# A two-part product at full TensorE load: the second weight part made by ScalarE and an accumulating transfer instead of VectorE

## The chip, the cores and the metric

One Trainium2 chip, one core of it. The metric is the device time of one execution in microseconds. The core has TensorE (matrix products, PE in the profile, PEld its weight loads), VectorE (DVE), ScalarE (ACT), GpSimd (POOL) and SyncE (SP), each with its own instruction stream, and 16 DMA engines that they share. Traces come from the hardware profiler.

## What is computed

Two layers of a generator block with four parallel branches (neighbourhood attention, pooling, grouped attention, convolution), over 256 latent tokens and, in layer 0, 256 context tokens as well; D is 2048. The weights make the bulk of the work: a combined input projection, four branch products with merge gates, and an output product.

```python
for l in range(DEPTH):
    shift, scale, gate = jnp.split(jax.nn.silu(c) @ w_ada[l] + b_ada[l], 3, axis=-1)
    h = modulate(x, g_pre[l], shift[:, None], scale[:, None])
    p = split_proj(h @ w_in[l])
    ...                                            # branches o_a, o_b, o_c, o_d
    y = branch_merge(p, o_a, o_b, o_c, o_d, w_branch[l], w_out[l])
    x = x + gate[:, None] * rms_norm(y, g_post[l])
```

## The kernel before

All products are of 32-bit numbers, and each operand is split in two parts, hi and lo, whose sum is the number. One product becomes three passes of TensorE: hi weights by hi activations, hi weights by lo activations, lo weights by hi activations (`mm3`, lines 164 to 167). The weights therefore arrive as a raw tile and are split on the chip.

The main stream is a list of *units*, each one raw weight tile of up to 1 MB (128 x 2048), and *steps*, each one half of a unit (128 x 1024): 24 passes of TensorE. In layer 0 the steps 96 to 165 are the input projection, 166 to 335 the four merges (pairs of a 1 MB unit of two steps for the gate, a 512 KB unit of one step for the branch product of two columns, and another 1 MB unit). In the steps of layer 0 a product mostly covers 512 columns, in layer 1 256.

`run` writes the order of every engine out by hand. Ahead of the products of step j it issues:

- `hi_op` for up to step j+3: ScalarE copies the raw half into a `wh` tile (line 279), a pool of four (`NHI`);
- `lo_op` for up to step j+2: VectorE subtracts, `wl = raw - wh` (line 286), a pool of three (`NLO`);
- behind the `lo_op` of a unit's last half, `dmas`: the raw tile of a unit that comes later, on SP's queue (line 237). There are three raw tiles (`NRAW`), and the load waits until the tile's earlier contents have been read;
- then the evacuation of the previous step (`post`), and ahead of each half of the step's products one or two *pulls*: pieces of side tasks (attention, convolution, pooling) and of a back task, the adaLN columns on VectorE (`ada_task`, from line 1051), which load 256 KB tiles `aw` on SP's queue (line 1061) one pull before VectorE multiplies them (lines 1098 and 1100).

Every engine takes its instructions in that order and waits where a tile is not ready or a buffer not free. GpSimd has next to nothing to do. PSUM has eight banks, from one pool.

Of the kernel before, what the change touches and what calls it, by code (L numbers as in the profile page):

```python
# [10 lines left out]
F32 = mybir.dt.float32  # L11
F32R = mybir.dt.float32r
AF = mybir.ActivationFunctionType
# [17 lines left out]
# column tiles of w_in, in the order in which the kernel consumes them  # L31
# [21 lines left out]
# columns of the table of per-feature parameters of a layer  # L53
# [9 lines left out]
class Step:  # L63
    __slots__ = ("unit", "half", "mm", "post", "pre", "pulls", "again", "cap")

    def __init__(self, unit, half, mm, post=None, pre=None, pulls=("", ""), again=False, cap=1.9):
        # again: the weights of this step are those that an earlier step of the unit has left
        # cap: the work that VectorE can take on in a pull, in us
        self.unit, self.half, self.mm, self.post, self.pre = unit, half, mm, post, pre
        self.pulls, self.again, self.cap = pulls, again, cap  # L70


class Unit:
    def __init__(self, src, widths, raw="raw", split="w", keep=False):
        # raw, split: where the loaded tile and its parts live; "u" is the common pool of 2 KB tiles
        # keep: a later step uses the parts again
        self.src, self.widths, self.keep = src, widths, keep
        self.rpool, self.spool = raw, split
        self.raw = None
        self.hi = {}  # L80
        self.lo = {}


class Kernel:
# [5 lines left out]
    EARLY = (6, 14)  # L90

# [20 lines left out]
    # ---- allocation  # L112
# [25 lines left out]
    # ---- small helpers  # L138
    def defer(self, fn):
        # emitted at the next quarter of a unit, so that an engine need not wait for what precedes it  # L140
        self.dq.append(fn)
# [6 lines left out]
    def spend(self, w):  # L148
        # one more operation of VectorE on w columns: is that enough for this pull?
        c = w * 0.00105 + 0.2  # L150
        self.spent += c
        if self.spent + c > self.cap:
            self.spent = 0
            return True
        return False

    def split(self, hi, lo, src, lag=False):
        # src = hi + lo exactly; both parts pass TensorE in one go each
        self.S.copy(hi, src)  # L159
        sub = lambda: self.V.tensor_tensor(lo, src, hi.bitcast(F32), ALU.subtract)  # L160
        self.defer(sub) if lag else sub()
# [23 lines left out]
    def tok_sums(self, acc, T, out):  # L185
        # out[:, 2j:2j+2] = the sum over partitions of token tile j, tokens on partitions
        accs = acc if isinstance(acc, list) else [acc]
        for j in range(T // 128):
            for i, a in enumerate(accs):
                self.T.matmul(out[:, 2 * j:2 * j + 2], a[:, j * 128:(j + 1) * 128], self.ones[:, 0:2],  # L190
                              start=i == 0, stop=i == len(accs) - 1)

    def tok_bcast(self, r, T, out, step=2):
        # out[p, t] = r[t] for every partition p
        for j in range(T // 128):
            self.T.matmul(out[:, j * 128:(j + 1) * 128], r[:, step * j:step * j + 1].to_broadcast([128, 128]),
                          self.ident, is_transpose=True)

    # ---- main program
# [8 lines left out]
    def pull(self, q):  # L208
        # the next piece of the first task; where that was a light one, one of the task behind it too
        i = 0  # L210
        while i < len(q):
            try:
                light = next(q[i])
            except StopIteration:
                del q[i]
                continue
            i += 1
            if not light:
                break
        return i > 0  # L220
# [18 lines left out]
    def run(self):  # L239
# [13 lines left out]
        def ahead(i, n):  # L253
            # may the split of step i be issued now? n: buffers of the pool of the weight parts
            # at the start, where the loads hold the time, what is split early would keep other work waiting
            if i >= len(prog) or i > self.j + (self.LOOK if self.j > self.SLOW else 1) or prog[i].unit.raw is None:
                return False
            if prog[i].again or prog[i].unit.spool == "u":
                return True
            # a kept tile is in use up to its last step  # L260
            return len({(id(p.unit), p.half) for p in prog[self.j:i + 1] if p.unit.spool == "w"}) <= n
# [19 lines left out]
        def lo_op(i):  # L281
            nonlocal busy
            x, h = prog[i].unit, prog[i].half
            if prog[i].again:
                return
            x.lo[h] = piece(i, self.lp, "wl", lambda d, r, k: self.V.tensor_tensor(  # L286
                d, r, x.hi[h][k].bitcast(F32), ALU.subtract))
            left[id(x)] -= 1
            if not left[id(x)]:
                busy -= x.rpool != "u"  # L290
                dmas()
# [39 lines left out]
    # ---- set-up  # L331
# [75 lines left out]
    # ---- the modulated, normalised input  # L407
# [10 lines left out]
    def startup(self):  # L418
        # scale and shift of layer 0 on TensorE, the first columns of its projection beside them
# [23 lines left out]
        def ada_post(g):  # L443
            def post():
# [3 lines left out]
                def cols():  # L448
# [7 lines left out]
                    def mods():  # L456
                        # stream 0: columns 0 and 1 of each tile, stream 1: columns 2 and 3
                        t = self.sm(16)
                        V.tensor_copy(t, pc[:, 0:16])
                        t4 = t.rearrange("p (j s h) -> p j s h", s=2, h=2)  # L460
                        V.tensor_tensor(t4[:, :, :, 0], t4[:, :, :, 0], t4[:, :, :, 1], ALU.add)
                        for i in range(2):
                            self.mod_cols(0, 2 * g + i, t4[:, 2 * i, :, 0], t4[:, 2 * i + 1, :, 0])
# [36 lines left out]
        for g in range(8):  # L500
            # between the last of a group and the first of the next, the bank of the sums serves for their columns
# [7 lines left out]
    # ---- projections  # L509
    def store(self, l, n, i, p):  # L510
        # p: PSUM tile of projection column tile i of part n
# [49 lines left out]
    def proj_mm(self, box, xh, xl, T, half, nk=8):  # L561
        # box: list to hold the PSUM tile; contraction tiles half*nk .. of the moving operand's pieces
# [18 lines left out]
    # ---- pooling branch  # L581
# [65 lines left out]
    # ---- convolution branch  # L647
# [84 lines left out]
    def conv_pw(self, l):  # L732
        # the pointwise product of the convolution branch, as a unit of the main stream
# [29 lines left out]
    # ---- attention  # L763
    def attn(self, units):
        # one pull per stage; what a stage reads was made at least one pull earlier
# [35 lines left out]
    def att_s(self, x):  # L801
        # q: the two parts of a head one above the other, kd, kl: the first and the second part of its keys, each twice
# [13 lines left out]
    def stack(self, src, w):  # L816
        # for each head of a pair, both parts of its 64 rows in one tile; the first part lies where the head lay
# [7 lines left out]
    def double(self, src):  # L825
        # for each head of a pair, the first part of its 64 rows twice, and the second part twice
# [12 lines left out]
    def vstack(self, p3, h):  # L839
        # values of a head, tokens on partitions: for each token tile the two parts side by side  # L840
# [25 lines left out]
    def att_tr(self, x, c):  # L866
        # key tiles 2c and 2c+1, both query tiles; ctx queries have only the keys of c = 1
# [81 lines left out]
    def attn_c(self, l):  # L949
# [7 lines left out]
        # tile 0: the keys of both groups, tiles 1 to 4: the queries; rows of ss: 8 query heads, then 2 groups  # L957
# [92 lines left out]
    # ---- adaLN columns on VectorE  # L1050
    def ada_task(self, kind):
# [11 lines left out]
        # sums over partitions as rows of one bank, a row for each group and stream  # L1063
# [71 lines left out]
    # ---- layers  # L1135
# [32 lines left out]
    def values(self, l, g):  # L1168
        # four contraction tiles of the values of branch a, tokens on the partitions of the result
# [16 lines left out]
        def post():  # L1186
            # for each head the two parts of its values side by side
# [83 lines left out]
    def layer_out(self, l):  # L1271
# [17 lines left out]
        def evac(f, box, streams):  # L1289
            # streams: those in the PSUM tile, one after the other  # L1290
# [48 lines left out]
        for f in range(NK):  # L1339
            # the last tiles of layer 0: first the latents, whose sums the next layer waits for, then the context  # L1340
# [9 lines left out]
    def load_x(self, g, s):  # L1350
        # feature tiles 2g and 2g+1 of stream s
# [4 lines left out]
    def sum_up(self, key, o, t):  # L1356
        # running sums over the feature tiles
# [7 lines left out]
    def tail0(self):  # L1365
        # the residual of layer 0, then the modulated input of layer 1; feature tiles in pairs
# [31 lines left out]
        def lat_task():  # L1398
            # the sum of the squares of x + r z from the sums over x x, x z and z z
# [169 lines left out]
# ---- host side: layout only  # L1569
def _tiles(w, cols):  # L1570
    # w: (rows, n) -> for each column tile in cols: (128 partitions, rows/128 * 128)
# [4 lines left out]
def _cols(v):  # L1576
    # feature vector -> (128, n/128), feature f at partition f % 128
    return v.reshape(-1, 128).T


def layout(inp):
    f32 = np.float32
    w_in, w_ada, w_out, w_br = inp["w_in"], inp["w_ada"], inp["w_out"], inp["w_branch"]
    a = {}
# [13 lines left out]
    def ada_cols(l, cols):  # L1598
        # columns in pieces of 128 -> (16 row blocks, 128, 512)
# [31 lines left out]
    # relative position bias: gathered by indices that depend on shapes alone, padded outside the window  # L1631
# [9 lines left out]
    # constants of the shapes  # L1641
# [48 lines left out]
```

## Time and profile before

| what | before |
|---|---|
| median of two runs | 2715.28 us (2715.2 to 2715.37) |
| span of the profiled execution, first to last instruction | 2712.6 us |
| TensorE busy | 2668.9 us, 98% |
| VectorE busy | 1880.6 us, 69% |
| ScalarE busy | 1187.7 us, 44% |
| all subtractions of line 286 | 720, 779.5 us |

The profile is one execution. Its own time is known as its span alone; the runs' median stands 2.7 us above that. "Busy" counts instructions that compute; products are pipelined and their ends modelled, so two neighbours overlap in the trace. A wait is written as the instruction that stood, an arrow, and what released it. DMA share is the mean busy share of the 16 DMA engines.

### The profile page before, as it was taken

What the parts mean: (1) busy time and instruction counts of PE and PEld (TensorE: products, weight loads), DVE (VectorE), ACT (ScalarE), POOL (GpSimd) and SP (SyncE); (2) the same over time, 40 slices, a digit from 0 to 9 for tenths busy, and PEclk for the clock granted to TensorE, in tenths of its full rate; (3) what the DMA queues carried; (4) which work ended last, traced back from release to release, by engine and by line L of the source; (5) the groups of instructions that cost most, each with busy time, mean ns of one, the idle gap of its engine ahead of it and who ended that gap; (6) DMA issues with size and microseconds to landing.
All of it is one profiled execution on the core that took longest, in us unless ns stands there. A gap on an engine that the chain in (4) does not pass through costs nothing.

```text
span 2712.6 us, 38481 instructions
## 1 busy us (share of the span) xinstructions
PE 2668.9 (98%) x15468; PEld 2320.9 (86%) x15468; DVE 1880.6 (69%) x2908; ACT 1187.7 (44%) x1866; POOL 0.2 (0%) x4
## 2 busy tenths in 40 slices
PE   6999999999999999999999999999999999999997
PEld 3678888788888888888888888899999999999997
DVE  8873667886487654677787565686787876875554
ACT  7852664345422223222222233466235764664443
POOL 0000000000000000000000000000000000000000
PEclk9999999999999999999999999999999999999999
DMA  8842224442232223445455355565335545445553
GB/s 333 294 165 101 88 101 152 148 145 81 83 119 94 100 94 109 148 171 198 168 171 184 118 197 200 186 222 187 109 115 175 179 150 175 148 149 183 185 186 119
DMA packets 106307, 422.42 MB, mean 156 GB/s; under 512 B 11624, under 2 KB 22288, under 8 KB 70416
## 3 DMA queue, kind: packets, MB, share of 16 engines
q1 hardware_dynamic: 106128, 419.96, 44.5%
q8 instruction: 121, 1.98, 0.3%
q14 instruction: 58, 0.48, 0.0%
HBM read 417.82 MB, written 2.10 MB: 155 GB/s over the span
## 4 chain that ended last, share of the span: by engine, by line
PE 94%; DVE 3%; ACT 2%; DMA 1%; issue 1%; SPq 0%; DVEq 0%; ACTq 0%
PE pm L165 23%; PE pm L166 23%; PE pm L167 23%; PE pb L165 3%; PE pb L167 3%; PE pb L166 3%; PE pk L165 1%; PE pk L166 1%; PE pk L167 1%; PE pt L872 1%; PE pv L166 1%; PE pv L167 1%; PE pv L165 1%; PE pa L440 1%; PE pa L439 1%; PE o L890 1%
## 5 line engine op out<-in xcount | busy, mean ns | idle before, releaser
L286 DVE TENSOR_TENSOR wl<-raw,wh 128x1024 fp32r<-128x1024 f32 (+1 forms) x720 | 779.5, 1098 | 668.6 <-PE pm L167 456.8
L279 ACT CAST wh<-raw 128x1024 fp32r<-128x1024 f32 (+1 forms) x720 | 671.1, 951 | 1282.0 <-PE pm L166 812.8
L165 PE MATMUL pm<-hh,wh 128*128 128x512 f32 (+1 forms) x3248 | 1097.4, 338 | 0.5 <-DVE tl L160 0.4
L167 PE MATMUL pm<-hh,wl 128*128 128x512 f32 (+1 forms) x3248 | 1088.1, 335 | 0.0
L166 PE MATMUL pm<-hl,wh 128*128 128x512 f32 (+1 forms) x3248 | 1087.8, 335 | 0.0
L165 PEld LDWEIGHTS pm<-hh,wh 128*128 128x128 f32 x3248 | 616.6, 190 | 65.3 <-issue 2.2
L167 PEld LDWEIGHTS pm<-hh,wl 128*128 128x128 f32 x3248 | 616.4, 190 | 62.7
L166 PEld LDWEIGHTS pm<-hl,wh 128*128 128x128 f32 x3248 | 616.9, 190 | 60.8
L1100 DVE SCALAR_TENSOR_TENSOR aacc<-aw,sc,aacc 128x512 f32<-128x512 f32 x420 | 291.1, 744 | 1.9 <-DMA aw<-in_adaD_dram 0.8
L165 PE MATMUL pm<-yh,wh 128*128 128x256 f32 (+1 forms) x544 | 177.9, 327 | 0.0
L167 PE MATMUL pm<-yh,wl 128*128 128x256 f32 (+1 forms) x544 | 177.7, 327 | 0.0
L166 PE MATMUL pm<-yl,wh 128*128 128x256 f32 (+1 forms) x544 | 177.7, 327 | 0.0
L672 DVE SCALAR_TENSOR_TENSOR cacc<-du,hlf,cacc 128x482 f32<-128x482 f32 (+29 forms) x240 | 145.1, 605 | 5.9
L165 PEld LDWEIGHTS pm<-yh,wh 128*128 128x128 f32 x544 | 103.5, 190 | 9.1
L166 PEld LDWEIGHTS pm<-yl,wh 128*128 128x128 f32 x544 | 103.5, 190 | 8.8
L167 PEld LDWEIGHTS pm<-yh,wl 128*128 128x128 f32 x544 | 103.5, 190 | 8.7
L858 ACT ACTIVATE P<-s,sm 128x512 f32<-128x512 f32 (+1 forms) x96 | 59.2, 617 | 92.8 <-DVE sm L857 87.3
L165 PE MATMUL pk<-hh,wh 128*128 128x256 f32 (+1 forms) x240 | 81.5, 339 | 0.1
L167 PE MATMUL pk<-hh,wl 128*128 128x256 f32 (+1 forms) x240 | 80.4, 335 | 1.1 <-DVE wl L286 1.1
L166 PE MATMUL pk<-hl,wh 128*128 128x256 f32 (+1 forms) x240 | 80.6, 336 | 0.5 <-DVE hl L160 0.5
L1239 DVE SCALAR_TENSOR_TENSOR mt<-mt,pb 128x512 f32<-128x512 f32 (+1 forms) x128 | 70.5, 551 | 11.8 <-ACT mt L1236 8.8
L160 DVE TENSOR_TENSOR tl<-pt,th 128x512 fp32r<-128x512 f32 x80 | 54.8, 686 | 18.8 <-ACT th L159 18.5
(277 smaller groups left out, 2912.5 us busy)
## 6 DMA issues: line engine op xcount, KB each, us to landing
raw<-in_wm_dram SPq DMA_DIRECT2D x229, 1024.0 KB, 4.9
aw<-in_adaD_dram SPq DMA_DIRECT2D x256, 256.0 KB, 5.4
raw<-in_ada_dram SPq DMA_DIRECT2D x32, 1024.0 KB, 5.0
raw<-in_wb_dram SPq DMA_DIRECT2D x64, 512.0 KB, 3.6
raw<-in_wv_dram SPq DMA_DIRECT2D x8, 1024.0 KB, 4.9
raw<-in_wk_dram SPq DMA_DIRECT2D x8, 1024.0 KB, 5.1
xr<-in_xT_dram SPq DMA_DIRECT2D x24, 256.0 KB, 5.4
x<-in_xT_dram SPq DMA_DIRECT2D x16, 256.0 KB, 5.0
```

The costliest lines, as they stand in the source:

```text
L160: sub = lambda: self.V.tensor_tensor(lo, src, hi.bitcast(F32), ALU.subtract)
L165: mm(out, wh, xh, start=first, stop=False)
L166: mm(out, wh, xl, start=False, stop=False)
L167: mm(out, wl, xh, start=False, stop=last)
L279: x.hi[h] = piece(i, self.hp, "wh", lambda d, r, k: self.S.copy(d, r))
L286: x.lo[h] = piece(i, self.lp, "wl", lambda d, r, k: self.V.tensor_tensor(d, r, x.hi[h][k].bitcast(F32), ALU.subtract))
L439: T.matmul(pa[g][0:4, :], w, hi[i], start=rb == 0, stop=False)
L440: T.matmul(pa[g][0:4, :], w, lo[i], start=False, stop=rb == 15)
L672: V.scalar_tensor_tensor(a3[:, :, lo:hi], u3[:, :, lo + d:hi + d], hlf[:, c:c + 1], a3[:, :, lo:hi], ALU.mult, ALU.add)
L858: S.activation(P[t], ss[t], AF.Exp, scale=0.125, bias=st[:, 2 + t:3 + t], accum_out=st[:, 4 + t:5 + t])
L1100: V.scalar_tensor_tensor(accs[s], w, c, accs[s], ALU.mult, ALU.add)
L1239: V.scalar_tensor_tensor(t, t, 1.0, q, ALU.add, ALU.mult)
```

## The change

For the steps 110 to 299, where the weight parts live in the pools `wh` and `wl`, `lo_op` no longer subtracts on VectorE. ScalarE writes the negated first part into the `wl` tile, and GpSimd issues a transfer within SBUF that adds the raw half (512 KB) to it. All else, the pools, the order and the conditions, stays as it was. (Comments were taken out as well; they are left out here.)

```diff
@@ class Kernel
     EARLY = (6, 14)
+    DLO = (110, 300)
@@ lo_op
-            x.lo[h] = piece(i, self.lp, "wl", lambda d, r, k: self.V.tensor_tensor(
-                d, r, x.hi[h][k].bitcast(F32), ALU.subtract))
+            if self.DLO[0] <= i < self.DLO[1] and x.spool == "w":
+                def low(d, r, k):
+
+                    self.S.activation(d, x.hi[h][k].bitcast(F32), AF.Copy, scale=-1.0)
+                    self.G.dma_start(d, r, accum_op=ALU.add)
+                x.lo[h] = piece(i, self.lp, "wl", low)
+            else:
+                x.lo[h] = piece(i, self.lp, "wl", lambda d, r, k: self.V.tensor_tensor(
+                    d, r, x.hi[h][k].bitcast(F32), ALU.subtract))
```

## Rows read from the trace of the kernel before

**Rows 1.** The page, part 1: engine, busy us (share of the span), instructions:
```profile
PE 2668.9 (98%) x15468; PEld 2320.9 (86%) x15468; DVE 1880.6 (69%) x2908; ACT 1187.7 (44%) x1866; POOL 0.2 (0%) x4
```

**Rows 2.** Windows: four stages of the stretch (columns: from:to, length, then as named):
```profile
core 0: us, PE busy (x) PEld busy (x) DVE busy (x) ACT busy (x) POOL busy (x), PEclk, DMA share, GB/s
240.00:400.00 160.00, 158.66 (x771) 132.97 (x770) 90.54 (x163) 88.39 (x164) 0.00 (x0) 1.00 0.26 93
400.00:610.00 210.00, 208.38 (x974) 169.67 (x972) 174.38 (x280) 92.62 (x157) 0.00 (x0) 1.00 0.43 151
610.00:1100.00 490.00, 489.99 (x2242) 406.40 (x2241) 306.85 (x450) 165.91 (x248) 0.00 (x0) 1.00 0.28 96
1100.00:1368.00 268.00, 268.00 (x1183) 220.36 (x1183) 199.00 (x265) 69.88 (x87) 0.00 (x0) 1.00 0.50 176
sum 1128.00, PE 1125.03 PEld 929.40 DVE 770.77 ACT 416.80 POOL 0.00; mean PE 281.26 PEld 232.35 DVE 192.69 ACT 104.20 POOL 0.00
```

**Rows 3.** The page, part 4: the chain that ended last, by engine:
```profile
PE 94%; DVE 3%; ACT 2%; DMA 1%; issue 1%; SPq 0%; DVEq 0%; ACTq 0%
```

**Rows 4.** Waits of TensorE's weight loads in the stretch: us, times, longest; first and last:
```profile
PEld o L890 <- DVE tl L160: 3.0, 5, 1.4
...
PEld pm L165 <- ACT mt L1236: 0.3, 1, 0.3
```

**Rows 5.** Groups of VectorE in the stretch: busy us, mean ns, idle before, releasers:
```profile
L286 DVE TENSOR_TENSOR wl<-raw,wh 128x1024 fp32r<-128x1024 f32 x190 | 232.4, 1223 | 300.3 <-PE pm L167 201.3 <-PE pb L167 42.5 <-issue 22.6
L1100 DVE SCALAR_TENSOR_TENSOR aacc<-aw,sc,aacc 128x512 f32<-128x512 f32 x272 | 186.0, 743 | 0.6 <-DMA aw<-in_adaD_dram 0.5
```

**Rows 6.** Windows: the same stages, the instructions of line 286 alone:
```profile
400.00:610.00 210.00, 40.14 (x33) 1.00 0.43 151
610.00:1100.00 490.00, 103.52 (x85) 1.00 0.28 96
1100.00:1368.00 268.00, 59.34 (x49) 1.00 0.50 176
```

**Rows 7.** Groups of ScalarE in the stretch:
```profile
L279 ACT CAST wh<-raw 128x1024 fp32r<-128x1024 f32 x190 | 200.3, 1054 | 632.8 <-PE pm L166 404.4 <-issue 106.4 <-PE pb L166 95.6
...
L864 ACT ACTIVATE P<-P,sm 128x512 f32<-128x512 f32 x32 | 21.4, 717 | 1.4 <-DVE sm L862 1.0
```

**Rows 8.** Timeline, 1303 to 1316: start, us, what, idle before; ScalarE, then VectorE:
```profile
1303.28 1.06 ACT L279 CAST wh<-raw 128x1024 fp32r<-128x1024 f32 x1 [3.94 <-issue]
...
1309.64 0.59 ACT L1236 ACTIVATE mt<-pm 128x512 f32<-128x512 f32 x1
...
1303.47 1.22 DVE L286 TENSOR_TENSOR wl<-raw,wh 128x1024 fp32r<-128x1024 f32 x1
...
1308.98 1.23 DVE L286 TENSOR_TENSOR wl<-raw,wh 128x1024 fp32r<-128x1024 f32 x1 [1.64 <-PE pm L167]
...
1314.35 1.23 DVE L286 TENSOR_TENSOR wl<-raw,wh 128x1024 fp32r<-128x1024 f32 x1 [2.67 <-PE pm L167]
```

**Rows 9.** SP's queue: its longest wait in the stretch; its issues after 1304:
```profile
SPq L237 <- DVE wl L286: 995.7, 107, 14.2
...
1304.75 0.33 SPq L237 DMA_DIRECT2D raw<-in_wm_dram  x1
1305.13 0.90 SPq L1061 DMA_DIRECT2D aw<-in_adaD_dram  x2
```

**Rows 10.** Transfers issued in the stretch: KB each, median us to landing:
```profile
raw<-in_wm_dram SPq DMA_DIRECT2D x81, 1024.0 KB, 4.9
aw<-in_adaD_dram SPq DMA_DIRECT2D x149, 256.0 KB, 5.3
raw<-in_wb_dram SPq DMA_DIRECT2D x26, 512.0 KB, 3.6
```

**Rows 11.** Transfers of the whole span: the only ones out of SBUF:
```profile
out_dram<-zg SPq DMA_DIRECT2D x8, 256.0 KB, 2.1
```

## The prediction, made before the changed kernel ran

> **What bounds the kernel now.** I read the page first. TensorE is busy for 98% of the span, VectorE for 69%, and POOL does four short instructions in all [rows 1]. The chain that ended last lies on TensorE for 94% of its length, on VectorE for 3% [rows 3]. Shares of busy time are averages, so next I cut out the stretch that the change touches. Between 240.3 and 1367 us VectorE makes exactly 190 second parts of 128x1024 [rows 5], which is one for each of the steps 110 to 299, about two steps ahead of its use. I split this into four stages [rows 2]: attention beside projections (240 to 400), the same with the adaLN columns (400 to 610), attention's end and two merges (610 to 1100), and merges with the adaLN columns (1100 to 1368). The reader should see three things there. TensorE is busy for 1125.03 of 1128.00 us, at the granted clock 1.00 (2.4 GHz) in each stage. VectorE is nowhere above 83%. And the DMA engines' share is not even: 0.26, 0.43, 0.28, 0.50.
>
> Third, the waits. TensorE's own and those of its weight loads come to little: of the nine rows of the weight loads the largest is 3.0 us and the smallest 0.3 [rows 4], 9.5 us together, partly the same idle time as the 2.97 us above. No row of them names a second part of the weights. VectorE in its turn stands idle for 300 us before the 190 subtractions, mostly because TensorE has not yet released the buffer [rows 5]. So the operation that the change takes away waits for TensorE, not TensorE for it.
>
> **The change, part by part.** *Removed:* 190 subtractions of 1223 ns, 232.4 us of VectorE [rows 5]. They lie under TensorE's work. What can come back is at most TensorE's idle time, 2.97 us, or 9.5 us if every wait of a weight load were real and gone. I take 0.
>
> *Added on ScalarE:* 190 copies with scale -1 on 128x1024. The nearest rows are the cast of the same shape, 1054 ns, and the scaled copy of half the width, 717 ns with its scale read from a tile [rows 7]. Twice the latter, 1.43, is the upper end; I take 1.05, which gives 200 us in 1128, so ScalarE goes from 417 to 617 us [rows 2], 55%. What stands behind it in ScalarE's order is the evacuation of the projection (590 ns at 1309.64, right behind the cast [rows 8]) and the exponentials of attention. They come 1.05 us later. Their cover is the pull of a later step that reads them, 5.44 us away. I count 0.
>
> *Added on POOL and the DMA engines:* 190 accumulating transfers of 512 KB within SBUF. Here is the core of the forecast: how long may one take? Take the merge stage [rows 8]. The subtractions start at 1303.47, 1308.98 and 1314.35, each when TensorE has let go of a buffer: two steps take 10.88 us, one 5.44. At 1303.47 the part for the step after next is made, in a pool of three. ScalarE first does its cast (from 1303.28, 1.06), then the new copy (1.05), and is done at 1305.39, 1.9 us after the release. TensorE needs the part when it is through with the two other buffers, at 1314.35. That leaves 1314.35 - 1305.39 = 9.0 us, call it the cover, for POOL's issue and the transfer's landing, D. The subtraction used 1.2 us of the same room.
>
> D has no row of its own, since nothing here accumulates and POOL issues no transfer. The nearest rows are plain ones [rows 10, 11]: 256 KB out of SBUF land in 2.1 us, 512 KB into it in 3.6, 1 MB in 4.9. From the last two, each 512 KB costs 1.3 us beside a fixed 2.3. Lower end: one pass, 3.6. An add has two operands to read, so I take the bytes twice, 4.9. A weight load that runs beside it shares the engines and adds at most its own 2.6 (4.9 - 2.3), which makes 7.5. The upper end is open, as no row tells what POOL needs to issue one. I take 5 alone and 7.5 beside a load. Both are below 9.0, so TensorE does not notice: 0.
>
> Of the engines' time: at 96 GB/s with a share of 0.28 [rows 2], full use would be 343 GB/s, so 512 KB are 1.5 us of all 16 engines, and twice that 3.0. Steps take 210/33 = 6.36, 490/85 = 5.76 and 268/49 = 5.47 us in the three later stages [rows 2, 6]. With 3.0 for each step the shares become 0.43 + 0.47 = 0.90, 0.28 + 0.52 = 0.80 and 0.50 + 0.55 = 1.05. Only the last goes over, by 5% of 268 us, 13 us; with 1.5 none does. The weights are loaded up to three units ahead, so some of this is absorbed. I take half: +7 us.
>
> A rule of the Trainium skill speaks against the change here. *Collectives: The Full Stack*, "The bandwidth ceiling: the fold count and why AG ≠ RS ≠ AR", says that an add inside the DMA engines costs nothing of itself but reads two sources, and gives 1.93 as the measured ratio of the copying collective's rate to the adding one's. No run so far shows it for this kernel. By that rule the last stage would be just over full, and this term about +13 us instead of +7.
>
> *Moved:* the weight load waits on SP's queue for the second part, since its buffer is then free. That wait is 995.7 us of the stretch, 107 times [rows 9]: SP is paced by little else. Now the subtraction ends at 1304.7 and the load goes out at 1304.75, with two adaLN loads behind it from 1305.13 [rows 8, 9]. With the change it goes out at 1305.39 + D, 1310.4 to 1312.9, that is 5.6 to 8.1 us later, and with it all that is queued behind: adaLN columns, biases. The weights themselves have room: a load of 4.9 us for parts that are cast three steps ahead, two units later. The adaLN columns have little. VectorE stands idle for only 0.6 us before their products in the whole stretch now [rows 5], and one takes 5.3 us to land [rows 10]. VectorE will wait for them every second step. In the last stage it can: 199.0 - 59.3 = 140 us of work in 268 [rows 2, 6] leave 5.2 us of every two steps. In 400 to 610 it is 174.4 - 40.1 = 134 in 210, 4.6 us of every two steps, and the wait may be above it. I count nothing for this in the sum, but it is half of the second rival.
>
> *Sum:* span 2712.6 - 0 + 0 + 7 = 2720, and 2.7 us lie around it (the median of the two runs, 2715.28, less the span; the execution's own time is not given apart). **2722 us.**
>
> **The rivals.** (A) *The forecast*: the transfer hides, 2706 to 2735.
>
> (B) *The engines or SP's queue are late a little.* By the shares, accumulates at 2.4 times the price of one pass (3.6 us of the engines) put the last stage at 0.50 + 0.66 = 1.16, +43 us. Or VectorE's wait for the adaLN columns in 400 to 610 exceeds its 4.6 us by 1.0 to 3.5 in 16 pairs of steps and reaches TensorE through ScalarE's exponentials: +16 to +56. For it: the queue in order and the 0.50. Against it: all these loads are behind buffers of several steps. 2735 to 2769.
>
> (C) *The other side: D exceeds the cover.* Then two steps take 1.9 + D instead of what TensorE needs. With 134 steps from 610 to 1368 at a mean of 758/134 = 5.66 us, 2% (54 us) are 0.40 for each step, so it decides from D = 2 x 6.06 - 1.9 = 10.2 us. With D = 12 a step takes 6.95: 134 x 1.29 + 33 x 0.59 = +192, 2907 us. The engines' time leads to the same end: at three passes, 4.5 us, the shares are 1.32 in the last stage, 1.14 from 400 to 610 and 1.06 between, +86 + 29 + 29 = +144. For it: no row has POOL issuing a transfer, and D of 7.5 beside a load uses most of the cover. Against it: 10.2 us is twice what a whole 1 MB load takes.
>
> (D) *TensorE's waits vanish and nothing is late*: 2715.3 - 9.5 = 2706. That is not 2% either: TensorE is not idle enough in this stretch.
>
> **How the numbers follow.** A 0.52, B 0.16, C 0.30, D's end over 2% 0.02 (only by something that I have not seen). 2%, 54 us, is about what a measurement of this kernel can tell from no change. So faster 0.02, same 0.52 + 0.16 = 0.68, slower 0.30. A's own range is 2706 to 2735. For eight in ten the range must take half of C as well: up to 2840, which is D of about 11.2 us. Range 2706 to 2840.
>
> **What would show it.** Right: in the stretch TensorE busy for all but a few us; its weight loads not waiting for the second part; from ScalarE's copy to landing 5 to 8 us; a DMA share of about 0.8 from 610 to 1100; SP's wait now ended by POOL's transfers. Wrong: idle time before the third product of each tile (line 167), released by a DMA; D of 9 or more; a stretch clearly longer than 1128 us at the same clock; or, for B, VectorE waiting for adaLN columns in 400 to 610 and ScalarE's exponentials waiting for VectorE behind it.

## The result: slower, 2781.3 us

The changed kernel takes 2781.3 us (two runs, 2780.96 to 2781.64) beside 2715.28: ratio 1.0241, 95% interval 1.0224 to 1.0258. The span of the profiled execution is 2779.2 us, 66.6 more than before. The forecast was 2722: the time is inside its range, but the kernel is slower by more than 2%, which the forecast gave 0.30.

The page of the kernel after, parts 1, 3, 4, 5 and 6, answers to [rows 1, 3, 5, 7, 10] (lines have moved: 280 is the cast, 290 the new copy, 291 the new transfer, 238 the weight load, 1069 the load of the columns, 166 to 168 the three passes):

```profile
PE 2691.7 (97%) x15468; PEld 2328.6 (84%) x15468; DVE 1662.7 (60%) x2718; ACT 1366.7 (49%) x2056; POOL 164.3 (6%) x194
...
q0 software_dynamic: 27360, 99.63, 18.6%
...
PE 60%; issue 29%; POOL 4%; DVE 2%; DMA 2%; ACT 2%; POOLq 0%; SPq 0%; ACTq 0%; DVEq 0%
...
L1108 DVE SCALAR_TENSOR_TENSOR aacc<-aw,sc,aacc 128x512 f32<-128x512 f32 x420 | 292.9, 747 | 169.0 <-DMA aw<-in_adaD_dram 167.5
L291 POOL DMA_DIRECT2D wl<-raw x190 | 164.1, 864 | 1264.5 <-ACT wl L290 1234.8
L290 ACT ACTIVATE wl<-wh 128x1024 fp32r<-128x1024 f32 x190 | 200.5, 1055 | 0.0
...
wl<-raw POOLq DMA_DIRECT2D x190, 512.0 KB, 6.0
aw<-in_adaD_dram SPq DMA_DIRECT2D x256, 256.0 KB, 5.8
```

VectorE has lost 218 us of work, and TensorE still has all the work it had, but 87.5 us of idle time instead of 43.7 (span less busy). The other 22.8 us of the loss are in its busy time: the same 15468 products took longer (roughly, as their ends are modelled). The wait that grew from nothing is VectorE's for the adaLN columns: 167.5 us before line 1108, where it was 0.8 in the whole span and 0.5 in the stretch [rows 5]. The chain tells less here than it seems to. It now runs through POOL's instructions, and "issue 29%" is the time between two of them, in which POOL (6% busy) waited for the next copy.

Windows of the same stages of work (attention beside projections; with the adaLN columns; attention's end; two merges; merges with the columns). They answer to [rows 2], whose third stage stands here in two parts:

```profile
240.00:410.00 170.00, 167.80 (x812) 139.82 (x811) 65.40 (x146) 114.98 (x197) 22.56 (x26) 1.00 0.68 167
410.00:660.00 250.00, 220.66 (x965) 175.99 (x964) 137.50 (x243) 121.63 (x186) 27.59 (x32) 0.94 0.76 199
660.00:774.00 114.00, 110.20 (x552) 92.21 (x552) 44.70 (x103) 76.38 (x138) 13.82 (x16) 1.00 0.59 143
774.00:1130.00 356.00, 353.84 (x1563) 290.38 (x1562) 149.23 (x235) 150.39 (x172) 55.26 (x64) 1.00 0.82 192
1130.00:1440.00 310.00, 301.42 (x1307) 243.81 (x1306) 160.14 (x242) 134.10 (x158) 44.86 (x52) 0.99 0.95 253
```

TensorE stands idle for 29.3 us in the second stage and 8.6 in the last; in the two where the DMA share is 0.59 and 0.82 and next to no columns load, for 3.8 and 2.2. The waits of the second stage, 410 to 660 (who stood, for whom: us, times, longest), name all 29.3 of it:

```profile
DVE aacc L1108 <- DMA aw<-in_adaD_dram: 37.1, 14, 6.9
...
PE o L898 <- DVE tl L161: 17.4, 8, 5.3
...
PE ss L980 <- DVE sql L161: 5.7, 1, 5.7
...
PE s L820 <- DVE qs L830: 5.1, 1, 5.1
...
PE pm L168 <- DMA wl<-raw: 1.1, 2, 0.6
```

17.4 + 5.7 + 5.1 are waits for small tiles that *VectorE* makes; only 1.1 us is a wait for the new weight part itself. So in this stage TensorE hardly waits for what was changed, but for an engine that has less to do than before. (In the last stage it is the other way round: there all 8.6 us are waits for the part, see below.) One place shows how, 439 to 455 (start, us, what, idle before and its end; first SP's queue, then POOL, VectorE, TensorE, its weight loads):

```profile
439.22 0.33 SPq L238 DMA_DIRECT2D raw<-in_wm_dram  x1
439.64 2.23 SPq L1069 DMA_DIRECT2D aw<-in_adaD_dram  x4
453.70 0.33 SPq L238 DMA_DIRECT2D raw<-in_wm_dram  x1
...
433.27 0.86 POOL L291 DMA_DIRECT2D wl<-raw  x1 [7.35 <-ACT wl L290]
439.21 0.86 POOL L291 DMA_DIRECT2D wl<-raw  x1 [5.08 <-ACT wl L290]
...
448.22 1.41 DVE L1108 SCALAR_TENSOR_TENSOR aacc<-aw,sc,aacc 128x512 f32<-128x512 f32 x2 [6.32 <-DMA aw<-in_adaD_dram]
...
451.54 1.27 DVE L161 TENSOR_TENSOR tl<-pt,th 128x512 fp32r<-128x512 f32 x2
...
447.66 0.28 PE L897 MATMUL o<-th,vs 128*128 128x256 f32 x1
452.27 0.58 PE L898 MATMUL o<-tl,vs 128*128 128x256 f32 x1 [4.33 <-DVE tl L161]
...
447.21 0.19 PEld L168 LDWEIGHTS pm<-hh,wl 128*128 128x128 f32 x1
...
454.57 0.34 PEld L166 LDWEIGHTS pm<-hh,wh 128*128 128x128 f32 x1
```

The transfer of 433.27 lands after 5.8 us. That releases the weight load (439.22), and the four columns behind it go out at 439.64. They share the engines with the load and the next accumulate and take 9.8 us, where the median was 5.3 [rows 10]. VectorE has nothing else to do from 441.9 and waits 6.32 us. Behind its four products, in order, stands `tl`, the second part of the attention weights, whose first part ScalarE had ready at 447.4. TensorE wants `tl` at 447.9 and gets it at 452.2. When it starts again its weight loads take 0.34 instead of 0.19 us: the granted clock has fallen to its lower level, 1.2 GHz. Windows of 50 us show how often (the eighth field, PEclk):

```profile
450.00:500.00 50.00, 39.97 (x167) 31.94 (x168) 23.67 (x38) 21.71 (x30) 5.17 (x6) 0.89 0.73 196
...
550.00:600.00 50.00, 44.86 (x193) 36.04 (x192) 34.78 (x67) 23.23 (x36) 6.03 (x7) 0.93 0.78 210
600.00:650.00 50.00, 42.17 (x196) 34.78 (x194) 21.96 (x45) 27.21 (x46) 5.17 (x6) 0.93 0.66 166
```

Before, this stage ran at 1.00 [rows 2]. It lost 41.2 us in all; TensorE's idle time rose from about 1.6 to 29.3, by 27.7, so that up to 13.5 are products that ran longer.

On SP's queue the weight load's wait (stretch 240 to 1440: us, times, longest) has changed its releaser, from VectorE [rows 9] to the transfer:

```profile
SPq L238 <- DMA wl<-raw: 1055.3, 113, 20.6
```

### The profile page after: what moved, and what is told of

Its sections match the earlier page's. It is cut to its first block, busy times and chain, and to the rows that moved or that the text cites. A ratio compares the mean times of both kernels' runs of the same rounds, so it can differ in the third digit from the quotient of the medians.

```text
span 2779.2 us, 39101 instructions
## 1 busy us (share of the span) xinstructions
PE 2691.7 (97%) x15468; PEld 2328.6 (84%) x15468; DVE 1662.7 (60%) x2718; ACT 1366.7 (49%) x2056; POOL 164.3 (6%) x194
## 3 DMA queue, kind: packets, MB, share of 16 engines
q0 software_dynamic: 27360, 99.63, 18.6%
## 4 chain that ended last, share of the span: by engine, by line
PE 60%; issue 29%; POOL 4%; DVE 2%; DMA 2%; ACT 2%; POOLq 0%; SPq 0%; ACTq 0%; DVEq 0%
PE pm L166 14%; PE pm L168 14%; PE pm L167 14%; POOL wl L291 4%; PE pb L166 2%; PE pb L168 2%; PE pb L167 2%; PE pk L166 1%; PE pk L167 1%; PE pk L168 1%; DMA wl<-raw 1%; PE pv L168 1%; PE pv L167 1%; PE pv L166 1%; PE pa L447 1%
## 5 line engine op out<-in xcount | busy, mean ns | idle before, releaser
L294 DVE TENSOR_TENSOR wl<-raw,wh 128x1024 fp32r<-128x1024 f32 (+2 forms) x530 | 547.3, 1053 | 364.2 <-PE pm L168 260.9
L166 PEld LDWEIGHTS pm<-hh,wh 128*128 128x128 f32 x3248 | 619.0, 191 | 66.6 <-issue 2.5
L1108 DVE SCALAR_TENSOR_TENSOR aacc<-aw,sc,aacc 128x512 f32<-128x512 f32 x420 | 292.9, 747 | 169.0 <-DMA aw<-in_adaD_dram 167.5
L291 POOL DMA_DIRECT2D wl<-raw x190 | 164.1, 864 | 1264.5 <-ACT wl L290 1234.8
L290 ACT ACTIVATE wl<-wh 128x1024 fp32r<-128x1024 f32 x190 | 200.5, 1055 | 0.0
```

What stands on the lines that cost most here:

```text
L166: mm(out, wh, xh, start=first, stop=False)
L290: self.S.activation(d, x.hi[h][k].bitcast(F32), AF.Copy, scale=-1.0)
L291: self.G.dma_start(d, r, accum_op=ALU.add)
L1108: V.scalar_tensor_tensor(accs[s], w, c, accs[s], ALU.mult, ALU.add)
```

## The experiments

Three theories of the 66.6 us. **Q**: the order on SP's queue; the columns stand behind a weight load that now waits for a landing. **E**: the DMA engines' time, which the transfer takes from the loads. **S**: ScalarE's extra 1.05 us for each step.

The table gives each kernel's loss against the kernel before in each stage, in us: from the start of the first product of one step to that of another, in the profiled execution of each, less the same of before. The steps' times in the kernel before stand in the first column; the parts ahead of step 110 and behind step 299 make up the rest to the span. Runs of one kernel lie up to 7 us apart, those of e9 16 us. The profiled one is the faster of two in e1 (2741.28), the slower in e2 (2759.32) and the slowest of four in e9 (2776.15). Part of the spread lies ahead of step 110, where nothing differs (5.0 us in e6). Each kernel was profiled once, so how much the loss of one stage varies from run to run is not shown.

| steps (us in before) | after | e1 | e2 | e3 | e4 | e5 | e6 | e7 | e8 | e9 |
|---|---|---|---|---|---|---|---|---|---|---|
| 110 to 133 (248 to 407), attention | 2.2 | 2.0 | 24.0 | 4.5 | 2.1 | 0 | 5.2 | 0.2 | 0 | 1.2 |
| 134 to 165 (407 to 614), with columns | 41.2 | 7.2 | 10.4 | 21.3 | 5.8 | 17.5 | 6.0 | 80.4 | 0 | 10.4 |
| 166 to 185 (614 to 748), attention's end | 4.9 | 4.9 | 9.7 | 1.3 | 4.8 | 0 | 5.9 | 0.3 | 0 | 1.2 |
| 186 to 245 (748 to 1077), merges | 3.4 | 2.8 | 0 | 0.6 | 2.8 | 0 | 0 | 4.4 | 3.7 | 13.5 |
| 246 to 299 (1077 to 1375), merges, columns | 13.8 | 8.1 | 0 | 52.2 | 17.5 | 31.0 | 0 | 98.4 | 0 | 34.9 |

The kernel before took 2715.67 us (median) beside e1 to e4, 2716.19 beside e5 to e7 and 2715.9 beside e8 and e9.

### e1: the same change, the weight load behind the step's pulls

```diff
         post = []
+        self.late = False
...
             if not left[id(x)]:
                 busy -= x.rpool != "u"
-                dmas()
+                if self.DLO[0] <= i < self.DLO[1]:
+                    self.late = True
+                else:
+                    dmas()
...
                 st.mm(hi, lo, part)
+            if self.late:
+                self.late = False
+                dmas()
```

> In the steps 110 to 299 the raw weight load is issued on SP's queue behind the products and pulls of its step instead of ahead of them, so the adaLN columns of that step no longer stand behind a load that waits for the accumulating transfer. All else is as in the changed kernel (2781.3 us). Theory Q (queue order: VectorE waits in order for the columns, TensorE for what VectorE has behind them): 2740 to 2762 us, VectorE's idle time before line 1108 falls from 169 us to under 100, steps 134 to 165 lose under 25 us instead of 41. Theory E (the DMA engines' time) and theory S (ScalarE's extra copy): 2777 to 2785, nothing of the kind changes.

Measured 2744.29 us (2741.28 to 2747.3), ratio 1.0106 [1.0076, 1.0135]: the order alone gives back 37 us, 34.0 of them in steps 134 to 165 (41.2 to 7.2). The columns do not land sooner after their issue (median in these steps 7.5 us, 6.7 in the change). They are issued sooner: counted from the start of the step in which the kernel before issued them, 3.2 us on average instead of 7.9, and 3.1 before. Waits of e1, 240 to 1440:

```profile
DVE aacc L1115 <- DMA aw<-in_adaD_dram: 135.5, 42, 8.6
...
PE o L905 <- DVE tl L161: 6.5, 9, 2.1
```

VectorE's wait only falls from 165.6 to 135.5 us (Q expected under 100), but TensorE's wait for `tl` falls from 20.8 to 6.5. In the steps 134 to 165 alone the two fall from 37.1 to 25.8 and from 17.4 to 3.2. What counts is not how long VectorE waits, but whether that is ahead of a tile that TensorE needs next. This speaks for Q: under E and S the time would have stayed at 2777 to 2785.

### e4: the same change, the columns on GpSimd's queue

```diff
-                self.nc.sync.dma_start(t, self.a["adaD"][g0 + g, rb])
+                e = self.G if self.DLO[0] <= self.j < self.DLO[1] else self.nc.sync
+                e.dma_start(t, self.a["adaD"][g0 + g, rb])
```

> The changed kernel, with the adaLN columns of the steps 110 to 299 loaded on POOL's queue, where they stand behind the issue of an accumulating transfer but not behind its landing. Theory Q: the columns are on time, steps 134 to 165 lose under 15 us instead of 41, 2735 to 2757 us in all. Theory E: as changed, 2775 to 2790 us, since the same bytes go through the same engines. Theory S: as changed.

Measured 2749.05 us (2748.97 to 2749.12), ratio 1.0123 [1.0094, 1.0153]. This is a second way out of SP's queue with the same effect where Q sits: 41.2 to 5.8 us in steps 134 to 165. In the last stage it costs 3.7 more than the change: GpSimd now issues two kinds of transfers in order, and the part itself comes late. Waits of e4, same stretch:

```profile
PE pb L168 <- DMA wl<-raw: 10.5, 5, 3.3
```

### e7: as before, but the weight load held until a transfer lands

VectorE subtracts as before. GpSimd, once the part is finished, issues an adding transfer that reads the raw half into the output's memory, which is overwritten at the end. The raw tile is free only when that has landed, so the load waits as in the change; TensorE waits for no transfer.

```diff
-                    self.S.activation(d, x.hi[h][k].bitcast(F32), AF.Copy, scale=-1.0)
-                    self.G.dma_start(d, r, accum_op=ALU.add)
+                    self.V.tensor_tensor(d, r, x.hi[h][k].bitcast(F32), ALU.subtract)
+                    self.G.tensor_copy(self.gate, d[:, 0:8].bitcast(F32))
+                    q = 512 * (i % 4)
+                    self.G.dma_start(self.out[q:q + 512, :].rearrange("(p r) t -> p (r t)", p=128), r,
+                                     accum_op=ALU.add)
...
+        self.gate = self.const("gate", 8)
```

> VectorE subtracts as before and TensorE and ScalarE have nothing new. When a second part is done, POOL issues an accumulating transfer of 512 KB that reads the raw tile (into memory that is overwritten at the end), so that the next weight load on SP's queue, and the columns behind it, wait for its landing as in the changed kernel. Theory Q: steps 134 to 165 lose 20 to 45 us with VectorE idle for the columns, 2735 to 2770 us in all. Theory E or S: no more than what a transfer without the held tile loses.

Measured 2897.89 us (2897.43 to 2898.35), ratio 1.0669 [1.0638, 1.07], far above the 2735 to 2770 that Q expected. Its waits, same stretch, SP's queue first:

```profile
SPq L238 <- DMA out_dram<-raw: 1075.9, 103, 17.6
...
DVE aacc L1111 <- DMA aw<-in_adaD_dram: 165.4, 27, 10.8
...
PE pm L168 <- DVE wl L289: 44.6, 12, 6.2
...
PE o L901 <- DVE tl L161: 30.7, 9, 10.5
```

e5, below, has a transfer of the same size that holds nothing. Holding the load costs 80.4 - 17.5 = 63 us more in steps 134 to 165, and 98.4 - 31.0 = 67 in the last stage; where next to no columns load, 0.2, 0.3 and 4.4 us are lost. So in steps 134 to 165 Q's mechanism is there by itself: no cast of ScalarE waits for a raw tile there, and of TensorE's waits 54.2 us are for VectorE's `tl`, `qs` and `sql`. In the last stage ScalarE's casts wait 170.1 us for raw tiles too, so the 67 us are not the columns' alone. That it costs more than in the change has a likely reason, which was not tried apart: a loop closes. VectorE waits for columns, subtracts late, and so the transfer, the load and the next columns are later still (counted as in e1, the columns of steps 134 to 165 go out 14.7 us after that start, 7.9 in the change). In the change the part is not VectorE's work, so the loop is open.

### e5: as before, with a transfer of the same size that nobody waits for

```diff
-                    self.S.activation(d, x.hi[h][k].bitcast(F32), AF.Copy, scale=-1.0)
-                    self.G.dma_start(d, r, accum_op=ALU.add)
+                    self.V.tensor_tensor(d, r, x.hi[h][k].bitcast(F32), ALU.subtract)
+                    q = 512 * (i % 4)
+                    self.G.dma_start(self.out[q:q + 512, :].rearrange("(p r) t -> p (r t)", p=128), d.bitcast(F32),
+                                     accum_op=ALU.add)
```

> VectorE subtracts as before the change and all tiles, pools and queues are as before it. Beside that POOL issues, for each of the 190 steps, an accumulating transfer of 512 KB from the finished second part into a part of the output's memory that is overwritten at the end; nothing but POOL waits for it. Theory Q (order on SP's queue): 2714 to 2722 us, and the columns are on time. Theory E (the engines' time alone): the steps 246 to 299 lose 8 us or more as in the changed kernel and its two variants (8 to 18), and 134 to 165 lose most of 41; 2723 to 2770 us.

Measured 2765.16 us (2763.46 to 2766.86), ratio 1.018 [1.0151, 1.021]. The issues of e5 in the stretch:

```profile
out_dram<-wl POOLq DMA_DIRECT2D x190, 512.0 KB, 8.1
...
aw<-in_adaD_dram SPq DMA_DIRECT2D x156, 256.0 KB, 10.0
```

The engines' time acts, but again through the columns: 17.5 and 31.0 us where they load, 0 in the other three stages, the merges of steps 186 to 245 at a DMA share of 0.90 among them. Q's 2714 to 2722 us are missed. The run overstates E: its transfers land in 8.1 us instead of 6.0 and the columns in 10.0 instead of 7.5, and VectorE still makes the part, for which TensorE waits 20.0 us, all in the last stage. The issues of the kernel after, same stretch:

```profile
aw<-in_adaD_dram SPq DMA_DIRECT2D x150, 256.0 KB, 7.5
```

How much of the change's loss is the columns' longer landing and how much their later issue, given both, stays open: e1 and e4 show that the late issue is needed for nearly all of the 34 us (in e1 the DMA share in these steps is 0.87, in the change 0.76), and no run had the late issue without the transfers' share of the engines.

### e3: a transfer beside the subtraction, inside SBUF

```diff
-    NHI, NLO, LOOK = 4, 3, 3
+    NHI, NLO, LOOK = 3, 3, 3
...
-                    self.S.activation(d, x.hi[h][k].bitcast(F32), AF.Copy, scale=-1.0)
-                    self.G.dma_start(d, r, accum_op=ALU.add)
+                    self.V.tensor_tensor(d, r, x.hi[h][k].bitcast(F32), ALU.subtract)
+                    self.G.dma_start(self.scr, x.hi[h][k].bitcast(F32), accum_op=ALU.add)
...
+        self.scr = self.const("scr", 1024)
+        V.memset(self.scr, 0.0)
```

> VectorE subtracts as before the change; beside it, for each of the 190 steps, POOL issues an accumulating transfer of the same 512 KB from the first part into a scratch tile that nobody reads. The weight load does not wait for it, nor does TensorE. For the scratch tile the pool of first parts has three buffers instead of four. Theory Q: 2714 to 2728 us; the engines are as busy as in the changed kernel, but nothing waits in order behind a transfer. Theory E: over half of the 66 us, 2748 to 2785 us, with the loss in the stages whose DMA share is 0.8 to 1.0.

Measured 2815.76 us (2814.63 to 2816.89), ratio 1.0369 [1.0339, 1.0399], but it made a wait of its own. The transfer reads the first part and so holds its buffer, of which there are only three here; waits of e3, same stretch:

```profile
ACT wh L280 <- DMA scr<-wh: 489.9, 105, 11.5
```

It has three such buffers outside the 190 steps too, and loses 21.7 us behind step 299. It says nothing on E; e5 was made in its place.

### e2: ScalarE's negated copy, then VectorE adds

```diff
-                    self.G.dma_start(d, r, accum_op=ALU.add)
+                    self.V.tensor_tensor(d, r, d.bitcast(F32), ALU.add)
```

> The changed kernel without its transfers: ScalarE writes the negated first part as there, and VectorE adds the raw half to it. Theory Q and theory E: 2714 to 2722 us, as before the change. Theory S (the 190 copies of 1.05 us on ScalarE lengthen the to and fro with VectorE in attention): steps 134 to 165 still lose 10 to 40 us, 2727 to 2757 us.

Measured 2755.71 us (2752.11 to 2759.32), ratio 1.0148 [1.0116, 1.0179], with no transfer at all. But VectorE now waits in order for each copy; waits of e2, same stretch:

```profile
DVE wl L291 <- ACT wl L290: 365.7, 167, 6.4
```

So it mixes S with a wait that neither kernel has. It does show that the merges (0 and 0) don't mind either.

### e6: as before, ScalarE casts each first part twice

```diff
-            x.hi[h] = piece(i, self.hp, "wh", lambda d, r, k: self.S.copy(d, r))
+            def cast(d, r, k):
+                self.S.copy(d, r)
+                if self.DLO[0] <= i < self.DLO[1] and x.spool == "w":
+                    self.S.copy(d, r)
+            x.hi[h] = piece(i, self.hp, "wh", cast)
...
-                    self.S.activation(d, x.hi[h][k].bitcast(F32), AF.Copy, scale=-1.0)
-                    self.G.dma_start(d, r, accum_op=ALU.add)
+                    self.V.tensor_tensor(d, r, x.hi[h][k].bitcast(F32), ALU.subtract)
```

> No transfer and VectorE subtracts as before, but in the 190 steps ScalarE makes its cast twice, one right behind the other into the same tile: 1.05 us more on ScalarE for each step, at the place of the changed kernel's copy, and nothing waits for a further result. Theory S in its weak form (the copy itself costs what is left where the columns play no part): the steps 166 to 185 lose about 5 us and 110 to 133 about 2, 2718 to 2728 us in all. Without theory S: 2714 to 2717 us. If the 41 us of steps 134 to 165 came from the copy: over 2740 us.

Measured 2734.52 us (2733.41 to 2736.7), ratio 1.0069 [1.0046, 1.0091], more than the 2718 to 2728 of S's weak form. The profiled execution loses 5 to 6 us in each of the three attention stages and 0 in the merges. Waits of e6, same stretch:

```profile
DVE tl L161 <- ACT th L160: 24.6, 26, 1.7
...
PE o L900 <- DVE tl L161: 8.2, 12, 2.2
```

In the kernel before VectorE waits 13.8 us for `th` and TensorE 1.6 for `tl`. So a late cast of the weights passes through `th` on ScalarE and `tl` on VectorE to TensorE, a microsecond at a time. S holds for attention's end: 5.9 us here, 4.9 in the change in steps 166 to 185. In 110 to 133 it costs 5.2 here, and the change loses 2.2 in all. In 134 to 165 its 6.0 would be nearly all that e1 and e4 leave (7.2 and 5.8), but that is by its size alone, and e9 does not bear it out.

### e9: the order of e1, and GpSimd makes the negated copy

The lines of e1 are in it as well; beside them:

```diff
-                    self.S.activation(d, x.hi[h][k].bitcast(F32), AF.Copy, scale=-1.0)
+                    self.G.tensor_scalar(d, x.hi[h][k].bitcast(F32), -1.0, None, ALU.mult)
```

> The changed kernel with the weight load issued behind the pulls of its step (so the columns are ahead of it on SP's queue) and with the negated copy made by GpSimd instead of ScalarE. ScalarE has then nothing more to do than before the change. Theory S (what is left in the attention stages is ScalarE's copy): steps 110 to 133, 134 to 165 and 166 to 185 together lose under 6 us instead of the 14 with the load behind alone; all in all 2722 to 2738 us, unless GpSimd's copy takes over 3 us and eats the cover, which would show as TensorE waiting for the transfer in the merges. Without theory S: the three stages lose 10 to 15 us as before, 2738 to 2746.

Measured 2771.29 us (2759.91 to 2776.15, four runs), ratio 1.0197 [1.0171, 1.0223]. Groups of e9 on POOL, same stretch:

```profile
L291 POOL TENSOR_SCALAR wl<-wh 128x1024 fp32r<-128x1024 f32 x190 | 541.5, 2850 | 652.4 <-issue 371.4 <-PE pv L167 237.7 <-DMA aw<-in_adaD_dram 11.1
L292 POOL DMA_DIRECT2D wl<-raw x190 | 170.6, 898 | 59.8 <-POOL wl L291 49.3 <-PE s L828 2.4 <-issue 2.3
```

With ScalarE free of the copy, steps 166 to 185 lose 1.2 instead of 4.9, as S says. Steps 134 to 165 lose 10.4, more than e1's 7.2, so the expectation for the three stages together was missed (12.8 us, not under 6), and that for the whole, 2722 to 2738, too. TensorE waits 4.3 us for `tl` there, 3.2 in e1, though ScalarE has no copy to make, and 5.6 for the part: S for these steps is not shown. The copy takes 2.85 us instead of 1.05, which is gone from the cover. In the merges TensorE now waits for the part itself, and they lose 13.5 and 34.9 us: rival C, on a small scale. Waits of e9, same stretch:

```profile
PE pm L168 <- DMA wl<-raw: 27.8, 17, 2.7
...
PE pb L168 <- DMA wl<-raw: 7.9, 8, 2.7
```

### e8: the change in steps 186 to 245 alone

```diff
-    DLO = (110, 300)
+    DLO = (186, 246)
```

> The change in the steps 186 to 245 alone: merges, no attention and no adaLN columns. The forecast's reading of the cover (9.0 us against a landing of about 6): 2716 to 2720 us, the stage loses under 5 us, no gain either since TensorE is full there. If the landing itself or the engines' time cost TensorE something everywhere: 2722 us or more.

Measured 2720.23 us (ten runs, 2718.01 to 2721.04), ratio 1.0016 [1.0006, 1.0025]; the stage loses 3.7 us in the profile. The median lies 0.2 us above the 2716 to 2720 of the forecast's reading and below the 2722 of the other. Who waited for the transfer of line 291 in e8, and its landing:

```profile
  PEld pb L168: 3.1, 4
  PE pb L168: 1.7, 1
...
DMA to landing us min/median/max: 4.5/6.2/9.7
```

Where next to no columns load and no attention runs, the forecast's reading of the cover holds: the transfers hide, but for the few that take close to the longest, and nothing is gained.

## Why the prediction was right and wrong

**Right.** *The work taken away was worth nothing:* 218 us less on VectorE bought no time in any stage. *The copy* takes 1055 ns (forecast 1.05 us). *The landing* has medians of 4.9 to 7.0 us by stage (forecast 5 and 7.5); but 28 of the 190 take over 9.0 us, 12 of them among the 52 of the last stage, and the longest 10.8. *The engines' time* of a transfer is 2.72 us (18.6% of 2779.2 us by 190), where I took 3.0. That is 1.8 times the 1.5 us of one pass. The Trainium skill (*Collectives: The Full Stack*, "The bandwidth ceiling: the fold count and why AG ≠ RS ≠ AR") tells of two source reads and a measured ratio of 1.93. The trace agrees roughly, with its 1.8. The shares came out as 0.76, 0.76 (0.59 and 0.82 in its two parts) and 0.95, forecast 0.90, 0.80 and 1.05; the stages are longer now, which lowers them. *The cover:* in the merges TensorE hardly waits for the part (e8: 3.7 us in 60 steps). And of the sign by which B was to be known the first half, VectorE waiting for the columns in the second stage, is there. That the time lies inside 2706 to 2840 is in part luck: it is above the forecast's own 2735 and B's 2769, and the range went on from there for C, whose mechanism cost at most 17 us here (3.4 + 13.8).

**Wrong: "I count nothing for this in the sum".** This was said of the weight load that goes out later, and the columns behind it. The load's delay was read rightly (5.6 to 8.1 us, from D of 5 to 7.5; the medians of the landing are 4.9 to 7.0), and so was VectorE's thin margin, 0.6 us of waiting in the whole stretch. But the margin was then weighed against VectorE's mean free time, 4.6 us of every two steps. VectorE works in order, and what decides is what stands behind the waiting product: `tl`, `sql` and `qs`. At 447.9, in the place shown, TensorE wanted `tl` 0.5 us after ScalarE had its first part ready. The term measured about 34 us (after less e1, steps 134 to 165). It belonged in the sum; rival B had the place, the sign and the size of this term (+16 to +56), at a chance of 0.16. B's path was off too: it goes through `tl` straight to TensorE, not through ScalarE's exponentials, whose wait for VectorE hardly moved in that stage (16.7 us, 14.2 before).

**Wrong: ScalarE's copy at 0.** I named the pull that reads the exponentials as their cover, 5.44 us away. For `th` there is no such cover: VectorE and TensorE take it up at once. Measured 5 to 6 us in each attention stage in e6; in the change 4.9 in the last of them, and up to 2.2 in the first.

**Too small: the last stage.** Forecast +7 from the engines' share, measured +13.8 at a share of 0.95. What failed here is the 0 for TensorE's wait: D was taken as 5 or 7.5 us, "Both are below 9.0". All of TensorE's idle time in this stage, 8.6 us, is its wait for the part, and the waits of its weight loads for the part come to 13.8. Waits of the kernel after, 1130 to 1440:

```profile
ACT wh L280 <- DMA raw<-in_wm_dram: 29.5, 7, 5.7
...
PEld pm L168 <- DMA wl<-raw: 13.8, 13, 2.8
PE pm L168 <- DMA wl<-raw: 8.6, 10, 2.4
```

Eight of the ten waits of TensorE stand behind landings of 9.4 to 10.8 us. That is C's mechanism, with a price of single microseconds. The other two, the longest among them, stand behind landings of 6.4 and 7.1 us, of parts that ScalarE began late, after it had stood 5.41 and 2.71 us for VectorE. Nor have the weights the room that the forecast gave them: ScalarE's casts wait 29.5 us for raw tiles, where none did in this stage before. e1 leaves 8.1 of the 13.8, so 5.7 go with the order; in e1 too TensorE waits for nothing but the part in these steps (5.6 us, 1096 to 1402).

**Not foreseen: the clock.** A pause of 4.33 us at TensorE was followed by products at half speed. No term had that; it is up to 13.5 us of the second stage, and most of it goes when the pauses go: in e1 the granted clock in steps 134 to 165 (411 to 625) is 0.99, and they lose 7.2 us altogether.

Together: about 34 (queue order in the second stage, the clock in it) + 6 (order in the last) + 14 (the copy and the rest in the attention stages, 2 + 7 + 5) + 8 (last stage, with the order of e1) + 3 (merges) + 1 (ahead of step 110) = 66.

No version here beats the kernel before, and none was in sight: TensorE is idle for 3 us of the stretch there, so there is nothing to win by relieving VectorE.

## What to carry to other kernels

When an operation moves from an engine to a transfer, list every queue on which something waits for its result, and what is queued behind that waiter: here a weight load held up the loads of an unrelated task. Compare the delay not with an engine's mean free time but with the slack of the next thing in its order that the bounding engine needs. And where the bounding engine is full, as here with 3 us of idle time in 1128, relieving another one has next to nothing to give back.

## What the hardware showed that I had not expected

- GpSimd needs 0.86 us to issue one adding transfer within SBUF of 512 KB, almost always the same (864 ns mean of 190); the landing spreads from 4.5 to 10.8 us.
- The same negated copy of 128x1024 takes 1.055 us on ScalarE and 2.85 us on GpSimd.
- A load of 256 KB landed in 5.3 us before, in 7.5 with these transfers on the engines, and in 10.0 in e5 (medians, 240 to 1440). The output's memory as their destination is not the reason by itself: in e7, which writes there too, it is 6.7.
- TensorE's granted clock, 1.00 in the whole stretch before, fell to 0.89 of full in the window 450 to 500, behind pauses like that of 4.33 us; e7, with TensorE busy for 1089.49 of the 1200 us from 240 to 1440, ran at 0.973 over its span.
